# A split-precision attention block on one core: part of its weight and bias loads issued by GpSimd in place of SyncE, and two numbers of the order tables

## The chip, the cores and the metric

The kernel runs on one core of a Trainium2 chip. The metric is the device time of one execution in microseconds (us). A core has five engines that run their own instruction streams in parallel: PE (TensorE; its weight loads are listed as PEld), DVE (VectorE), ACT (ScalarE), POOL (GpSimd) and SP (SyncE, which here only issues DMA transfers). DMA transfers run beside them.

## The reference

```python
h = rms_norm(x, norm_gain)                       # x: 2048 tokens x 1024
qa, ka, va, qb, kb, vb, ga, gb, mg = split(h @ w_in)
ya = banded_attention(rms(qa), rms(ka), va, 128, stride 1, bias, sink)   # 8 heads, 2 kv heads
yb = softmax-weighted sum over 3 groups of banded_attention(...)          # (window, dilation)
#    = (128, 1), (512, 4), (2048, 16), 8 heads each
ya, yb = ya * silu(ga), yb * silu(gb)
gates = sigmoid(mg + b_merge)
merged = gates[0] * (ya @ w_branch_a) + gates[1] * (yb @ w_branch_b)
out = x + merged @ w_out
```

All of it is in float32. The kernel reaches that accuracy on PE with pairs of fp16 numbers: each operand is a high half and a low half, and a product takes three matmuls (high by high, high by low, low by high).

## The kernel before

**Three stages.** In the first 80 us x is loaded, normalised, transposed and split into XH and XL, which stay in SBUF, and the gates of branch A are made. From 80 to about 1232 us the attention runs, with the gates of branch B and pieces of other work between. From there to the end is the tail: merge gates, the two branch projections and the output projection, as seven-product matrix multiplications.

**Units and pairs.** The attention is cut into 14 units (two of kind A, twelve of kind B, in the order A, B, A, B, B, B ...), each a group of heads with weights of its own (1024 x 384, float32, 1.5 MB) and a bias table (768 KB for A, 256 KB for B). A unit has 8 pairs, each two blocks of 128 tokens: 112 pairs of about 10 us. For a pair PE makes q, k and v (L693). ACT, DVE and POOL then norm q and k: ACT squares them, DVE sums, POOL refines the reciprocal root (L266 to L269), DVE scales (L753), POOL multiplies by the gain (L760), ACT makes the high halves (L766), DVE the low ones (L770), POOL copies them swapped (the "swap" copy, L775, into the tile spl). SP then issues a transpose through DMA, kq<-spl (L783 for A, L786 for B). PE makes the scores from kq (L846), DVE adds the bias and takes maxima (L861), ACT and DVE make the probabilities in two halves (L874, L878), SP issues their transpose, pt<-p (L884), and PE multiplies them by v (L895). POOL also sets a column of each v tile (L722, "vt") and works on the merging of heads (L1037, L1058), whose operands come by a load zz<-zd (L904).

**Weights.** The raw float32 weights of the unit after the present one go into the one raw tile, wraw, by four DMAs of 384 KB, in two twos (w_load, L180). ACT squares them (L215), PE sums (L191), DVE makes a scale from the sum, ACT makes the high halves and DVE the low ones (L238). After that the raw tile is free; from unit 3 on, eight units each put 1 MB of the branch and output weights there for a sum of squares (window, piece_load L1083 and L1086, piece_square L1090), before the next unit's weights come. Bias tables are loaded at the start of a unit (bias_load, L664 and L667). In the tail the same raw tile takes the merge gates' weights, "gate weights" below.

**What sets the order.** Each engine executes its instructions in the order in which the program writes them. In the attention that is set by a heap: at(t, f) places a step at a time counted in pairs, and tables hold the times (NORM for the steps of the norm, W_STEP for the weights: loads .1 and .6 pairs after a unit's start, squares from 1.9 on). W_SOON is subtracted from the loads' and squares' times for one unit alone, number 2, the second A unit. In the tail a planner places the steps by estimated times; G_LD is the lag that it assumes between the start and the landing of the first gate weights, and so decides when their squares and the matmul that sums them are written.

**DMAs.** Every DMA above is issued by SP, so that all are on one queue. SP's stream is in order: a transpose behind a load is issued after it.

Of the kernel before, what the change touches and what calls it, by code (L numbers as in the profile page):

```python
# [45 lines left out]
def unit_order():  # L46
    us = [("A", 0, 0)]
    for p in range(4):
# [9 lines left out]
NU = len(UNITS)  # L58
# [10 lines left out]
Y_PART = (-0.02, 0.571, 0.797, 0.981, 1.031)  # L69
GATE = (-0.062, 0.084, 0.255)  # L70
W_STEP = (0.1, 0.6, 1.9, 0.445, 4.186, 0.117, 0.301)
W_SOON = (1.9, .5)
W_MAX = (3.542, 3.596)
G_PREP = (5.907,)
N_PREP = (5.948, 6.756, 7.277)
# [4 lines left out]
            sum=.76, yl=7.0, cp=.66, pl=6.0, a2=.44, h2=.51, l2=.5)  # L80
SEQ = ((1, 0), (1, 1), (8, 0), (8, 1), (2, 0), (2, 1), (9, 0), (9, 1), (3, 0), (3, 1), (10, 0), (10, 1), (4, 0), (4, 1),
       (5, 0), (5, 1), (6, 0), (6, 1), (7, 0))
G_T0, G_LD, G_SQ = 5.0, 3.0, 2.0
W_RAW, L_LAST = 14.0, 0.4
STD, W_EARLY, G_TH, G_SI, G_CP, K_AT = 5.2, 24.0, 2.0, 4.0, 1.0, (4, 17)
Y_S = 4.0
# [24 lines left out]
def block_kernel(tc, x, w_units, w_gate, w_mrg, w_out, w_bra, w_brk, gain, qkg, sink, bias_a, bias_b, b_merge, out):  # L111
    nc = tc.nc
# [52 lines left out]
    def raw_tile():  # L165
        return wp.tile([128, NCH, 384], F32, name="wraw", bufs=1)
# [7 lines left out]
    def w_load(u, parts=(0, 1, 2, 3)):  # L174
        if u not in wtiles:
            wtiles[u] = [raw_tile()]
        raw = wtiles[u][0]
        src, n = (w_units[u], 384) if u < NU else (w_mrg[u - NU], 256)
        for i in parts:
            nc.sync.dma_start(out=raw[:, 2 * i:2 * i + 2, :n], in_=src[:, 2 * i:2 * i + 2, :])  # L180


    held = [False, True]
# [366 lines left out]
    n = 0  # L550
    for k in X_LD:
        for i in range(4 if k == "u" else 1):
            f, args = {"g": (gain_load, ()), "u": (w_load, (0, (i,)))}.get(k, (x_load, (k,)))
            if k in ("w0", "w1"):
                f, args = g_load, (int(k[1]),)
            at(.001 * n, f, *args)
            od.end["ld", k, i] = us_["land"] + us_["next"] * n
            n += 1
            if n == 8:
                at(.001 * n, small_loads)  # L560
    od.add("gs", "V", us_["gs"], [("ld", "g", 0)], 0, gain_scale)
    for t in range(NT):
# [9 lines left out]
        for h in range(2):  # L572
            k = 2 * t + h
# [53 lines left out]
    class Unit:  # L627
# [31 lines left out]
        def bias_load(self):  # L659
            big = self.u % 2 == 0  # L660
            b = bp.tile([128, 4, N_BIAS_A] if big else [128, 4, 128], F32, name=f"b{self.u % 2}")
            if self.kind == "A":
                self.bias = b
                nc.sync.dma_start(out=b[:], in_=bias_a[self.idx])  # L664
            else:
                self.bias = b[:].rearrange("p a b -> p (a b)")[:, :2 * N_BIAS_B].rearrange("p (a b) -> p a b", a=2)
                nc.sync.dma_start(out=self.bias[:], in_=bias_b[self.idx, self.g])  # L667

        def bias_scale(self):
            V.tensor_scalar(self.bias[:], self.bias[:], NSIG[self.br][:], None, OP.mult)  # L670
# [403 lines left out]
    pre = {}  # L1074
# [5 lines left out]

    def piece_load(u, k):
        if k < 4:
            nc.sync.dma_start(out=pre[u][1], in_=w_bra[k])  # L1083
        else:
            h, i = divmod(k - 4, 2)
            nc.sync.dma_start(out=pre[u][1].rearrange("p (a b) -> p a b", b=512), in_=w_out[h, :, 4 * i:4 * i + 4, :])  # L1086

    def piece_square(u, k, half):
        v = pre[u][1][:, 1024 * half:1024 * half + 1024]
# [87 lines left out]
    def w_forms(u, t):  # L1177

        r = []

        def split():
            raw, s, inv, _, _ = wtiles[u]
            wh, wl = (w[:].rearrange("p (f c n) -> p f c n", f=7, c=4) for w in wfull[u])
            v = raw[:, :, :256]
            r.extend((s, *w_sums(v[:, 0:4, 0:128], v[:, 0:4, 128:256], v[:, 4:8, 0:128], v[:, 4:8, 128:256],
                                 lambda t: t[:].rearrange("p (c n) -> p c n", c=4), lambda: sb_p.tile([128, 512], F32, name="sr")), wh, wl))
            wtiles[u, "forms"] = wh, wl
            std_im(u - NU)

        def hi(i):  # L1190
            A.activation(r[3][:, i], r[1][i], AF.Copy, scale=r[0][:])

        def lo(i):
            V.scalar_tensor_tensor(r[4][:, i], r[1][i], r[0][:], r[3][:, i], OP.mult, OP.subtract)

        at(t + F_AT[0], split)
        for i in range(4):
            at(t + F_AT[0] + .01 + F_AT[1] * i, lambda i=i: r[2][i]())
        for i in range(7):
            at(t + F_AT[2] + F_AT[3] * i, hi, i)  # L1200
            at(t + F_AT[2] + F_AT[3] * i + F_AT[4], lo, i)
        at(t + F_AT[5], w_load, NU + SEQ[2][0])
# [8 lines left out]
    for u in range(NU + 1):  # L1211
        t = 8 * u
        ahead = W_SOON if u == 1 else (0.0, 0.0)
        steps = [(t + W_STEP[i] - ahead[0], w_load, u + 1, (2 * i, 2 * i + 1)) for i in range(2)]
        for i in range(4):
            steps.append((t + W_STEP[2] + W_STEP[3] * i - ahead[1], w_square, u + 1, i))
            if u < NU:
                steps += [(t + W_STEP[4] + W_STEP[3] * i, w_hi, u + 1, i),
                          (t + W_STEP[4] + W_STEP[5] + W_STEP[3] * i, w_lo, u + 1, i)]
        chain(steps + [(t + d, f, u + 1) for d, f in zip(W_MAX, (w_sum, w_pow))])  # L1220

    for k in range(8):
        u = 3 + k
        t = 8 * u
        at(t + G_PREP[0] - .01, window, u)
        at(t + N_PREP[0], piece_load, u, k)
        for half in range(2):
            at(t + N_PREP[1 + half], piece_square, u, k, half)
# [7 lines left out]
    while t < NPAIR or heap or any(k >= t for k in fill):  # L1236
        u, j = divmod(t, 8)
# [676 lines left out]
    class Branch(Seven):  # L1914
        n, mm_us = 7, MM1
# [65 lines left out]
    class Out(Seven):  # L1981
        n, mm_us = 7, MM
# [77 lines left out]
    for s in range(8):  # L2060
        p = pos[0]
# [92 lines left out]
```

## Time and profile before

| | |
|---|---|
| time, median of 3 runs (lowest to highest) | 1905.94 us (1905.17 to 1907.07) |
| the profiled execution's own time; its span | 1904.35 us; 1902.3 us |
| PE, DVE, ACT, POOL busy | 98%, 79%, 66%, 30% of the span |
| granted clock of PE | 1.00 |
| DMA engines busy, mean of the attention | 0.84 |
| weight loads of the units (L180): number, size, time to landing | 56, 384 KB, 4.8 us |
| bias loads of B (L667) | 12, 256 KB, 3.6 us |

The profile lists, for groups of instructions, busy time and the idle time of the engine ahead of them with what ended it (the releaser). The chain of waits follows the work that ended last back from the end. A timeline row has start, busy time, engine, line, operation, tile written <- tiles read, sizes and count, and in brackets the idle time ahead with its releaser. SPq stands for the issuing of DMAs by SP.

### The profile page before, as it was taken

The page shows a single profiled execution, that of the slowest core. Times are in us where ns is not written, and L with a number is a line of the kernel's source. Part 1 is how long each engine was busy: PE and PEld are TensorE (multiplying, and loading weights), DVE is VectorE, ACT ScalarE, POOL GpSimd, SP SyncE. Part 2 cuts the span into 40 slices and gives each one's busy share as a digit, 9 for nine tenths or more (in the row PEclk, how much of TensorE's full clock was granted, in tenths as well). Part 3 has the DMA queues.
Part 4 walks back from the last instruction along what each step waited for, and adds up shares of the span by engine and source line. Part 5 has one row for each costly group of instructions (what it writes and reads, how often), then busy time and mean ns, then how long its engine had stood idle before and what let it go on. Part 6 is the DMA issues. An engine that isn't in the chain of part 4 may idle for free.

```text
span 1902.3 us, 51104 instructions
## 1 busy us (share of the span) xinstructions
PE 1869.9 (98%) x19254; PEld 1439.0 (76%) x19254; DVE 1499.3 (79%) x3837; ACT 1249.5 (66%) x3015; POOL 579.6 (30%) x1363
## 2 busy tenths in 40 slices
PE   6999999999999999999999999999999999999999
PEld 4567987889999899998999899544444446776775
DVE  7689879986886888878789888748779644987885
ACT  8477768886777776777777766565666865433341
POOL 0133433443463435544454444300000000322121
PEclk9999999999999999999999999999999999999999
DMA  6259998988888679878897777776666648854452
GB/s 257 83 107 199 168 198 138 201 163 156 168 149 180 139 158 201 146 165 173 145 176 149 147 148 134 170 303 183 204 199 188 192 150 272 297 164 120 144 151 74
DMA packets 638983, 326.21 MB, mean 171 GB/s; under 512 B 458768, under 2 KB 589712, under 8 KB 636304
## 3 DMA queue, kind: packets, MB, share of 16 engines
q1 hardware_dynamic: 638592, 322.69, 73.4%
q8 instruction: 150, 2.46, 0.6%
q14 instruction: 97, 0.79, 0.1%
q10 hardware_dynamic: 144, 0.26, 0.0%
HBM read 139.08 MB, written 73.66 MB: 112 GB/s over the span
## 4 chain that ended last, share of the span: by engine, by line
PE 89%; DMA 5%; ACT 2%; DVE 2%; issue 1%; POOL 0%; SPq 0%; DVEq 0%; POOLq 0%; ACTq 0%
PE pj L693 42%; PE fps L1607 18%; PE fps L1927 8%; PE fps L2012 7%; PE s L846 5%; PE pv L895 4%; DMA pt<-p 2%; DMA kq<-spl 2%; PE pj L306 2%; PE pj L354 1%; PE fps L306 1%; ACT jk L443 1%; PE pt L959 1%; DMA bigl<-sd 1%; PE s L484 0%
## 5 line engine op out<-in xcount | busy, mean ns | idle before, releaser
L693 PE MATMUL pj<-wl,XH 128*128 128x128 f16 (+2 forms) x2816 | 715.2, 268 | 0.0
L693 PE MATMUL pj<-wh,XL 128*128 128x128 f16 (+2 forms) x2816 | 711.7, 269 | 0.0
L693 PE MATMUL pj<-wh,XH 128*128 128x128 f16 (+2 forms) x2816 | 708.6, 268 | 0.0
L693 PEld LDWEIGHTS <-XH 128*128 128x128 f16 x5632 | 574.9, 112 | 54.2
L693 PEld LDWEIGHTS <-XL 128*128 128x128 f16 x2816 | 315.8, 112 | 23.8
L861 DVE CUSTOM_DVE_ANT_0 pr<-s,b,ubuf 128x256 f32<-128x256 f32 (+3 forms) x512 | 219.0, 465 | 40.7 <-PE s L846 38.1
L878 DVE SCALAR_TENSOR_TENSOR p<-pr,p 128x512 f16<-128x512 f32 (+2 forms) x256 | 194.9, 761 | 47.9 <-ACT p L874 46.4
L760 POOL TENSOR_TENSOR rw<-rw,g 128x128 f32<-128x128 f32 (+1 forms) x224 | 149.2, 686 | 195.2 <-DVE rw L753 174.8
L1937 POOL TENSOR_TENSOR g<-g,t 128x512 f32<-128x512 f32 x32 | 48.4, 1512 | 522.1 <-DVE t L1859 521.6
L1607 PEld LDWEIGHTS <-wh 128*128 128x128 f16 x1064 | 104.2, 99 | 123.5 <-issue 0.5
L711 ACT ACTIVATE rw<-pj 128x256 f32<-128x256 f32 (+1 forms) x224 | 87.4, 390 | 134.5 <-PE pj L693 134.0
L775 POOL COPY spl<-spl 128x256 f16<-128x256 f16 (+1 forms) x224 | 96.4, 459 | 244.6 <-DVE spl L770 244.6
L874 ACT ACTIVATE p<-pr 128x512 f16<-128x512 f32 (+2 forms) x256 | 157.6, 616 | 11.9 <-DMA pt<-p 7.4
L846 PE MATMUL s<-kq 128*128 128x128 f16 (+1 forms) x1984 | 151.3, 217 | 5.9 <-DMA kq<-spl 4.7
L1927 PE MATMUL fps<-y,bigh 128*128 128x128 f16 x1792 | 153.4, 219 | 0.0
L1927 PE MATMUL fps<-y,bigl 128*128 128x128 f16 x896 | 151.7, 219 | 0.0
L846 PEld LDWEIGHTS <-kq 128*128 128x128 f16 x2016 | 131.0, 98 | 22.2 <-issue 7.2
L2012 PE MATMUL fps<-WO,mf 128*128 128x512 f16 x660 | 147.5, 379 | 0.0
L1927 PEld LDWEIGHTS <-bigh 128*128 128x128 f16 x1792 | 139.0, 98 | 7.3
L895 PE MATMUL pv<-vt,pt 128*128 128x65 f16 (+1 forms) x2784 | 131.6, 193 | 4.3 <-DMA pt<-p 4.1
L895 PEld LDWEIGHTS <-pt 128*128 128x128 f16 x3024 | 119.5, 97 | 19.6 <-DMA pt<-p 7.1
L766 ACT ACTIVATE spl<-rw 128x512 f16<-128x512 f32 (+1 forms) x112 | 72.0, 643 | 79.1 <-POOL vt L722 67.2
(255 smaller groups left out, 3803.5 us busy)
## 6 DMA issues: line engine op xcount, KB each, us to landing
wraw<-in_w_units_dram SPq DMA_DIRECT2D x56, 384.0 KB, 4.8
g<-mgd SPq DMA_DIRECT2D x64, 256.0 KB, 5.0
wraw<-in_w_mrg_dram SPq DMA_DIRECT2D x45, 256.0 KB, 4.3
mgd<-t SPq DMA_DIRECT2D x43, 256.0 KB, 2.8
zd<-z SPq DMA_DIRECT2D x128, 66.0 KB, 2.1
zz<-zd SPq DMA_DIRECT2D x64, 132.0 KB, 3.3
xt<-in_x_dram SPq DMA_DIRECT2D x16, 512.0 KB, 7.8
ytd<-yo SPq DMA_DIRECT2D x32, 256.0 KB, 3.3
```

Source lines behind the costliest of these rows:

```text
L693: out.append(lambda lhs=lhs, rhs=rhs, ch=ch, a=a, b=b, k=k: T.matmul(ps[:, a:b], lhsT=lhs[:, ch, :], rhs=rhs[:, ch, a:b], start=(k == 0), ...
L711: A.activation(self.rw[:, n * i:n * i + n], self.ps[i][:, :n], AF.Copy)
L760: G.tensor_tensor(q[:, i, :un.nq, :], q[:, i, :un.nq, :], g, OP.mult)
L775: G.tensor_copy(sp[:, i, nh:, :, :], sp[:, i, nq:nh, ::-1, :])
L846: T.matmul(self.sv[j][:, o:o + k1 - k0], lhsT=q[:, h, :], rhs=kt[:, un.nq + kh + v * un.nk, k0:k1], start=(v == 0), stop=(v == 1))
L861: V.tensor_tensor_reduce(out=self.pv[:, j, self.p0:self.p0 + W], in0=self.sv[j], in1=un.bias[:, self.h0 + j, self.b0:self.b0 + W], scale=I ...
L874: A.activation(self.sp[:, :128 * n], self.pr, AF.Copy, scale=PSC)
L878: V.scalar_tensor_tensor(self.sp[:, 128 * n:], self.pr, PSC, self.sp[:, :128 * n], OP.mult, OP.subtract)
L895: T.matmul(self.po[:, j, :w], lhsT=p[:, n * j + s, :], rhs=un.v[key][:, vh, c0:c0 + w], start=(k == 0 and s == 0), stop=(k == 2 and s == n ...
L1607: T.matmul(b[k][:], lhsT=w[:, i, ch, :], rhs=xform(PROD[i][0], lo, ch, q), start=(i < 3 and n == 0), stop=(n == 11), skip_group_check=True)
L1927: out.append(lambda p=p, c=c, wl=wl, yl=yl, n=n: T.matmul(ps[:, 128 * p:128 * p + 128], lhsT=w[wl][:, i, c, p, :], rhs=y[:, yl, c, :], sta ...
L2012: out.append(lambda p=p, ml=ml, wl=wl, k=k: T.matmul(ps[:], lhsT=m[:, ml, p, :], rhs=WO[:, i, wl, p, :], start=(fresh and k == 0), stop=(k ...
```

## The change

Three edits. W_SOON goes from (1.9, .5) to (0, 0): unit 2's loads come 1.9 pairs later, its squares half a pair later, as those of every other unit. G_LD goes from 3.0 to 6.0. And 74 DMAs are issued by GpSimd in place of SP: the weights of units 1 to 13 (52), the bias tables (14) and the eight pieces of 1 MB. The weights of unit 0 and the gate weights of the tail stay with SP.

```diff
-W_SOON = (1.9, .5)
+W_SOON = (0.0, 0.0)
...
-G_T0, G_LD, G_SQ = 5.0, 3.0, 2.0
+G_T0, G_LD, G_SQ = 5.0, 6.0, 2.0
...  w_load
         for i in parts:
-            nc.sync.dma_start(out=raw[:, 2 * i:2 * i + 2, :n], in_=src[:, 2 * i:2 * i + 2, :])
+            (nc.gpsimd if 0 < u < NU else nc.sync).dma_start(out=raw[:, 2 * i:2 * i + 2, :n], in_=src[:, 2 * i:2 * i + 2, :])
...  bias_load
-                nc.sync.dma_start(out=b[:], in_=bias_a[self.idx])
+                nc.gpsimd.dma_start(out=b[:], in_=bias_a[self.idx])
...
-                nc.sync.dma_start(out=self.bias[:], in_=bias_b[self.idx, self.g])
+                nc.gpsimd.dma_start(out=self.bias[:], in_=bias_b[self.idx, self.g])
...  piece_load
         if k < 4:
-            nc.sync.dma_start(out=pre[u][1], in_=w_bra[k])
+            nc.gpsimd.dma_start(out=pre[u][1], in_=w_bra[k])
         else:
             h, i = divmod(k - 4, 2)
-            nc.sync.dma_start(out=pre[u][1].rearrange("p (a b) -> p a b", b=512), in_=w_out[h, :, 4 * i:4 * i + 4, :])
+            nc.gpsimd.dma_start(out=pre[u][1].rearrange("p (a b) -> p a b", b=512), in_=w_out[h, :, 4 * i:4 * i + 4, :])
```

The first place is SP's stream at the first two pairs of unit 5, a B unit (at 510 us in the trace of before). Before, the bias load (b) and the four weight loads stand between the transposes:

```order
L884 DMA_TRANSPOSE pt_9544<-p_9481 128x8x128
L667 DMA b_9557<-in_bias_b_dram 128x512
L180 DMA wraw<-in_w_units_dram 128x768 x2
L904 DMA zz<-zd_82 128x2x132 x2
L786 DMA_TRANSPOSE kq<-spl 128x6x128 x2
L884 DMA_TRANSPOSE pt_9675<-p_9602 128x8x128
L180 DMA wraw<-in_w_units_dram 128x768 x2
L976 DMA ytd<-yo 128x512
L884 DMA_TRANSPOSE pt_9788<-p_9723 128x8x128
```

Now the same stretch of SP's stream is:

```order
L884 DMA_TRANSPOSE pt_9544<-p_9481 128x8x128
L904 DMA zz<-zd_82 128x2x132 x2
L786 DMA_TRANSPOSE kq<-spl 128x6x128 x2
L884 DMA_TRANSPOSE pt_9675<-p_9602 128x8x128
L976 DMA ytd<-yo 128x512
L884 DMA_TRANSPOSE pt_9788<-p_9723 128x8x128
L904 DMA zz<-zd_82 128x2x132 x2
```

The five loads are gone from it; each kq and pt is the next DMA behind what was ahead of the loads.

The second place is the same stretch on POOL. Before, from the gain of unit 5's first pair to the gain of its second:

```order
L760 TENSOR_TENSOR rw<-rw,g_857 128x128 x2
L722 MEMSET vt 128x2
L775 COPY spl<-spl 128x256 x2
L266 TENSOR_TENSOR rs_t<-rs_y 128x8
L267 TENSOR_TENSOR rs_t<-rs_t,qss 128x8
L268 TENSOR_SCALAR rs_t<-rs_t 128x8
L269 TENSOR_TENSOR qr<-rs_t,rs_y 128x8
L1058 TENSOR_TENSOR zz<-zz,bm_e 128x4x64 x3
L722 MEMSET vw 128x2
L1037 COPY zz<-nmB 128x4
L760 TENSOR_TENSOR rw<-rw,g_857 128x128 x2
L722 MEMSET vt 128x2
```

Now:

```order
L760 TENSOR_TENSOR rw<-rw,g_857 128x128 x2
L667 DMA b_9557<-in_bias_b_dram 128x512
L722 MEMSET vt 128x2
L180 DMA wraw<-in_w_units_dram 128x768 x2
L775 COPY spl<-spl 128x256 x2
L266 TENSOR_TENSOR rs_t<-rs_y 128x8
L267 TENSOR_TENSOR rs_t<-rs_t,qss 128x8
L268 TENSOR_SCALAR rs_t<-rs_t 128x8
L269 TENSOR_TENSOR qr<-rs_t,rs_y 128x8
L1058 TENSOR_TENSOR zz<-zz,bm_e 128x4x64 x3
L722 MEMSET vw 128x2
L180 DMA wraw<-in_w_units_dram 128x768 x2
```

The bias load and two weight loads stand ahead of the swap copy L775 of the first pair, and the other two ahead of the merge's copy L1037 (which comes next there) and the gain L760 of the second.

The third place is PE at the start of the tail, where matmuls on XH and XL (the first product) are followed by those on bigh and bigl (sums of blocks of h, loaded from DRAM). The norm matmul L191 sums the squares of the first gate weights of the planner. Before:

```order
L1607 MATMUL fps<-XL,wh 128x512
L1607 LDWEIGHTS wl
L1607 MATMUL fps<-XH,wl 128x512
L191 MATMUL fps<-wsq,ones 128x4
L1607 LDWEIGHTS wh
L1607 MATMUL fps<-bigh,wh 128x512
L1607 LDWEIGHTS wh
L1607 MATMUL fps<-bigl,wh 128x512
L1607 LDWEIGHTS wl
```

Now, twelve matmuls later:

```order
L1607 MATMUL fps<-bigh,wh 128x512
L1607 LDWEIGHTS wh
L1607 MATMUL fps<-bigl,wh 128x512
L1607 LDWEIGHTS wl
L1607 MATMUL fps<-bigh,wl 128x512
L191 MATMUL fps<-wsq,ones 128x4
L1607 LDWEIGHTS wh
L1607 MATMUL fps<-bigh,wh 128x512
L1607 LDWEIGHTS wh
```

L191 went from ahead of the first twelve matmuls on bigh and bigl to behind them. DVE and ACT change by a few rows there.

## The prediction

> **What bounds the kernel now.** First the head of the profile, with the busy shares, then the DMA queues and issues.
>
> ```profile
> span 1902.3 us, 51104 instructions
> PE 1869.9 (98%) x19254; PEld 1439.0 (76%) x19254; DVE 1499.3 (79%) x3837; ACT 1249.5 (66%) x3015; POOL 579.6 (30%) x1363
> q1 hardware_dynamic: 638592, 322.69, 73.4%
> wraw<-in_w_units_dram SPq DMA_DIRECT2D x56, 384.0 KB, 4.8
> wraw<-in_w_bra_dram SPq DMA_DIRECT2D x4, 1024.0 KB, 6.1
> kq<-spl SPq DMA_TRANSPOSE x208, 3.6
> ```
>
> PE is busy 98% of the span, so an edit gains only what it takes out of the 32 us in which PE is not busy, and loses only where it makes PE wait. Nearly all bytes go through one queue, q1, which SP fills; the loads that the change moves (384 KB and 1024 KB) stand in it beside the transposes (pt and kq) that the attention waits for. The table by stage says where PE is idle: preparation, attention, the passage to the tail, the tail. After the time its columns are PE, PEld, DVE, ACT, POOL (us, instructions), granted clock, DMA share and GB/s.
>
> ```profile
> 0.00:80.00 80.00, 62.05 (x333) 37.78 (x334) 59.26 (x120) 57.94 (x107) 1.96 (x10) 1.00 0.44 170
> 80.00:1230.00 1150.00, 1139.84 (x13815) 1014.25 (x13813) 961.86 (x2805) 839.23 (x2246) 507.27 (x1305) 1.00 0.84 162
> 1230.00:1250.00 20.00, 18.91 (x88) 8.27 (x86) 9.25 (x20) 12.10 (x23) 0.00 (x0) 1.00 0.90 327
> 1250.00:1899.00 649.00, 649.00 (x5024) 378.67 (x5022) 468.43 (x892) 340.20 (x640) 70.33 (x48) 1.00 0.60 185
> PE s L846 <- DMA kq<-spl: 4.7, 5, 1.4
> PE pv L895 <- DMA pt<-p: 4.1, 5, 1.3
> ```
>
> The clock is full throughout. Of 1150 us of attention PE is idle for 10.2, and the last two rows (PE's waits in that stretch: total, times, longest) say for what: 4.7 + 4.1 = 8.8 us for transposes. That is the most the attention can give. The tail after 1250 has no idle time at all, and the passage has 1.1 us. The 18 us at the start end before the first moved load matters. Which of the ten waits stand behind a moved load is read from PE's timeline (start, busy, then in brackets the idle time ahead and its releaser) and SP's.
>
> ```profile
> 150.56 0.61 PE L846 MATMUL s<-kq 128*128 128x128 f16 x8 [1.42 <-DMA kq<-spl]
> 152.77 0.41 PE L895 MATMUL pv<-vt,pt 128*128 128x65 f16 x8 [1.12 <-DMA pt<-p]
> 180.72 0.44 PE L895 MATMUL pv<-vt,pt 128*128 128x65 f16 x9 [1.35 <-DMA pt<-p]
> 500.53 0.49 PE L846 MATMUL s<-kq 128*128 128x128 f16 x6 [0.94 <-DMA kq<-spl]
> 530.75 0.44 PE L846 MATMUL s<-kq 128*128 128x128 f16 x5 [1.01 <-DMA kq<-spl]
> 745.37 0.49 PE L846 MATMUL s<-kq 128*128 128x128 f16 x6 [0.44 <-DMA kq<-spl]
> 970.28 0.49 PE L846 MATMUL s<-kq 128*128 128x128 f16 x6 [0.94 <-DMA kq<-spl]
> ```
>
> ```profile
> 142.41 1.37 SPq L180 DMA_DIRECT2D wraw<-in_w_units_dram  x2
> 143.83 2.62 SPq L783 DMA_TRANSPOSE kq<-spl  x1
> 146.63 5.42 SPq L884 DMA_TRANSPOSE pt<-p  x2
> ...
> 489.93 0.35 SPq L1083 DMA_DIRECT2D wraw<-in_w_bra_dram  x1
> ...
> 493.61 5.37 SPq L786 DMA_TRANSPOSE kq<-spl  x2
> ...
> 511.66 0.57 SPq L667 DMA_DIRECT2D b<-in_bias_b_dram  x1
> 512.28 2.45 SPq L180 DMA_DIRECT2D wraw<-in_w_units_dram  x2
> ...
> 515.81 2.56 SPq L786 DMA_TRANSPOSE kq<-spl  x2
> 518.47 1.25 SPq L884 DMA_TRANSPOSE pt<-p  x1
> 519.77 1.06 SPq L180 DMA_DIRECT2D wraw<-in_w_units_dram  x2
> ```
>
> A transpose behind a load is issued late and lands late: 142.41 loads, then the kq and pt of 143.83 and 146.63, and PE waits at 150.56 and 152.77. The same pattern precedes 500.53 (a 1 MB load at 489.93) and 530.75 (loads at 512.28 and 519.77).
>
> **The change, part by part.** The working is against the profiled execution's own 1904.35 us (span 1902.3 and 2.05 around it); the median of the runs shown, 1905.94, is 1.59 more, which is added at the end.
>
> *Unit 2's loads (W_SOON).* They leave 142 and 152, so the two waits there should go: -(1.42 + 1.12) = **-2.5**, at worst 0. They come back 1.9 pairs later, around 163 and 171, and run beside transposes near the 1.35 wait at 180.72. I charge **+1.0** there; the ends are 0 and the +2.5 that the same four loads cost at 142. The squares on them start half a pair later; nothing waits, since unit 2's weights are needed a whole unit on.
>
> *The other loads leave SP's queue.* The waits at 500.53, 530.75, 745.37 and 970.28 add to 0.94 + 1.01 + 0.44 + 0.94 = 3.33. I take **-3.0** (ends -3.3 and 0): the transposes are then issued at once, yet share the 16 engines with the same bytes, so a rest stays.
>
> *What POOL pays.* No row shows a load issued by POOL. SP's direct loads cost it 1.06/2 = 0.53 us each, its transposes 1.25, and if POOL were held until the load landed it would be the 4.8 of the issues. So c, POOL's time for one issue, lies between 0.53 and 4.8; I take 1.0, between the two issue costs, since a plain load is an issue and not a transfer on its engine. POOL's timeline shows the cover:
>
> ```profile
> 492.96 0.74 POOL L775 COPY spl<-spl 128x256 f16<-128x256 f16 x2 [1.87 <-DVE spl L770]
> ...
> 512.27 0.74 POOL L775 COPY spl<-spl 128x256 f16<-128x256 f16 x2 [2.47 <-DVE spl L770]
> ...
> 518.83 1.17 POOL L760 TENSOR_TENSOR rw<-rw,g 128x128 f32<-128x128 f32 x2 [1.16 <-DMA zz<-zd]
> ...
> 522.91 0.74 POOL L775 COPY spl<-spl 128x256 f16<-128x256 f16 x2 [2.86 <-DVE spl L770]
> ```
>
> In a unit's first pair, a bias load and two weight loads go ahead of the swap copy L775, where POOL idles 2.47: 3c = 3.0 makes the copy 0.5 late. That copy ends at 512.27 + 0.74 = 513.01, while SP issues its kq only at 515.81, 2.80 later, behind the loads. With these gone the copy may be 2.80 late before kq is later than now: c can reach (2.47 + 2.80)/3 = **1.76** free of charge. In the second pair two loads stand ahead of L760: 2c = 2.0 against 1.16, and the 0.84 over it falls into the 2.86 of idle time ahead of 522.91. A piece load is c = 1.0 against 1.87. So **0**, with the loss beyond 1.76 kept as a rival.
>
> *Waits that come to POOL with the loads.* Each waits for the raw tile; behind it on POOL are the vt memset, the swap copy, and the kq transpose that waits for the copy.
>
> ```profile
> 69.47 1.01 DVE L238 SCALAR_TENSOR_TENSOR wl<-wraw,ubuf,wh 128x768 f16<-128x768 f32 x1
> 89.81 0.20 POOL L266 TENSOR_TENSOR rs_t<-rs_y 128x10 f32<-128x10 f32 x1 [26.83 <-ACT rs_y L258]
> 488.85 1.01 DVE L238 SCALAR_TENSOR_TENSOR wl<-wraw,ubuf,wh 128x768 f16<-128x768 f32 x1
> 498.24 1.05 ACT L1090 ACTIVATE wraw<-wraw 128x1024 f32<-128x1024 f32 x1
> ```
>
> The tile is free when the last low half is made: at 70.48 for unit 1, with POOL idle until 89.81, and at 489.86 for the 1 MB piece, before POOL reaches its idle time at 492.96 - 1.87 = 491.09, where the piece load now stands. So no wait. That piece, issued about 491.1 + 1.0 and landing 6.1 later, comes at 498.2, just as ACT's square at 498.24 wants it; a little lateness there holds ACT, not PE, whose 500.53 wants kq.
>
> *The tail (G_LD).* The only PE row that moves is the norm matmul of the first gate weights, now behind the twelve matmuls on bigh and bigl.
>
> ```profile
> 1241.60 0.39 PE L191 MATMUL fps<-wsq,ones 128*128 128x4 f32 x2 [0.99 <-ACT tq L1457]
> 1237.82 9.92 DMA bigl<-sd
> 1247.79 25.84 PE fps L1607 x119
> ```
>
> PE waits 0.99 there for the squares. But the chain of waits does not run through it: it goes through the last bigl landing at 1247.74, after which PE never idles. Taking the norm away moves the matmuls on bigh and bigl earlier, and they then wait for their landings instead. **0**, with -1.0 as the other end.
>
> Sum: 1904.35 - 2.5 + 1.0 - 3.0 + 0 + 0 = 1899.85; with 1.59, **1901.4**.
>
> Two rules of the Trainium skill speak against parts of this. "DMA: Bandwidth & Descriptors", section "Issuing engines are not separate DMA queues", says that loads from any engine end on the same 16 DMA engines, so that another issuer saves only issue time; the trace's one queue cannot show it, and by it the -3.0 would shrink to little: that is the second rival. "SBUF — State Buffer", section "SBUF: two separate sides", says that a load issued by GpSimd needs descriptors written by GpSimd, which is locked out while VectorE runs in a two-port mode, and gives 620 ns alone and 3100 ns beside VectorE; an estimate from that page is 3 x 3.1 = 9.3 us against 5.27 of cover, and 12 times the difference, 48 us, for the kernel. No run here shows it; the first rival is priced without it.
>
> **The rivals.**
>
> *POOL held by its issues (slower).* The place is L775 in the first pair of each unit; it decides from c = 1.76. At c = 2.5: 3 x 2.5 - 2.47 - 2.80 = 2.23 us that kq lands later than now, at each of the 12 unit starts whose loads stand so (units 1 to 12, each loading its own bias and the next unit's weights): +26.8. The kq gains are then gone, those at 150 remain: 1904.35 - 2.5 + 26.8 + 1.59 = **1930**. For it: DVE is busy 962 of the 1150 us beside POOL, and no row bounds c below 1.76. Against it: both issue costs that the trace has are lower, and PE may have more slack than I grant.
>
> *The engines stay shared (no change).* The DMA engines are busy 0.84 of the attention, and the moved bytes are the same. If collisions only move (a kq at 500 instead of one at 530), the -3.0 becomes 0 and +1.0 becomes +2.5: 1904.35 - 2.5 + 2.5 + 1.59 = **1906**. For it: the pt wait at 180.72 and others stand behind no load. Against it: every kq wait does.
>
> *The tail's wait goes too (faster).* The 0.99 is really saved: 1901.4 - 1.0 = **1900.4**. Against it stands the chain through bigl.
>
> **How the numbers follow.** About 0.2% (3.8 us) is what a measurement of this kernel can tell from no change, so faster is below 1902.1 and slower above 1909.8. The forecast has 0.40; its own range runs from 1899.1 (-2.5, 0, -3.3, -1.0) to 1902.9 (+2.5 in place of +1.0), so 0.30 of it is faster and 0.10 the same. The tail case has 0.07, faster. Engines shared has 0.23, the same. POOL held has 0.30: 0.18 up to the price at c = 2.5, 0.12 above. Faster 0.37, same 0.33, slower 0.30. The range goes down to the attention's whole 8.8 (1904.35 - 8.8 + 1.59 = 1897.1) and up to 1930, which leaves out about 0.12 above and little below.
>
> **What would show it.** Right: the waits at 150, 500, 530, 745 and 970 are gone, kq is issued within 0.3 us of its copy, and POOL's rows at 512 have at most 0.5 us of new lateness. Wrong by POOL: idle time ahead of L775 that "issue" or a load ends, kq's issue waiting for L775 for over 2.8 us, and new PE waits for kq in the first pair of every unit. Wrong by shared engines: kq is issued early, but its time to landing grows past the 3.6. At the tail PE should wait for bigh or bigl in place of L191.

## The result, and the profile after

The change makes the kernel slower: 1923.79 us, median of five runs (1920.9 to 1952.06), against 1905.94; the ratio is 1.0116 with a 95% interval of 1.0094 to 1.0138. The ratio is that of the means, without the longest run, which is over 1.5% above the fastest. The forecast was 1901.4, on the other side of no change. The profiled execution of the changed kernel is that longest one (1952.06 us, mean clock 0.991); a second profile of the same kernel (1931.25 us) is used beside it.

The head of the profile after, its DMA queues and its DMA issues:

```profile
span 1950.3 us, 51177 instructions
PE 1882.9 (97%) x19254; PEld 1445.1 (74%) x19254; DVE 1500.0 (77%) x3837; ACT 1247.9 (64%) x3015; POOL 619.9 (32%) x1437
q1 hardware_dynamic: 627936, 289.13, 67.8%
q0 software_dynamic: 6560, 33.56, 6.7%
wraw<-in_w_units_dram POOLq DMA_DIRECT2D x52, 384.0 KB, 7.0
wraw<-in_w_out_dram POOLq DMA_DIRECT2D x4, 1024.0 KB, 8.3
kq<-spl SPq DMA_TRANSPOSE x208, 3.7
```

The 74 loads, 33.56 MB, are now on a queue of their own, q0. POOL has 74 more entries and 40.3 us more busy time: 40.3/74 = 0.54 us for one issue, at the lower bound of the prediction (0.53). The unit weights now take 7.0 us to land in place of 4.8. The median transpose hardly changed (3.6 to 3.7), which hides what happened to a few. PE's waits say it (line, what it waited for, total, times, longest):

```profile
PE s L846 <- DMA kq<-spl: 22.5, 6, 7.8
PE pv L895 <- DMA pt<-p: 21.7, 8, 5.5
```

8.8 us of waits for transposes became 44.2, so 35.4 more; PE's busy time went from 1869.9 to 1882.9, 13.0 more. Together that is 48.4 of the 48.0 us by which this span is longer. The second profile gives the same account, with waits of 19.8 + 7.1 = 26.9 (18.1 more) and 1879.1 busy (9.2 more) against a span 27.2 longer:

```profile
span 1929.5 us, 51177 instructions
PE 1879.1 (97%) x19254; PEld 1443.7 (75%) x19254; DVE 1502.9 (78%) x3837; ACT 1246.9 (65%) x3015; POOL 621.1 (32%) x1437
PE s L846 <- DMA kq<-spl: 19.8, 7, 5.5
PE pv L895 <- DMA pt<-p: 7.1, 6, 2.5
```

One site shows the mechanism. Here is POOL, then SP, then PE in the changed kernel around 1080 us, where a B unit starts:

```profile
1075.43 0.59 POOL L667 DMA_DIRECT2D b<-in_bias_b_dram  x1
1076.03 0.13 POOL L722 MEMSET vt<- 128x2 f16 x1
1076.07 1.06 POOL L180 DMA_DIRECT2D wraw<-in_w_units_dram  x2
1077.58 0.74 POOL L775 COPY spl<-spl 128x256 f16<-128x256 f16 x2 [0.45 <-DVE spl L770]
...
1081.60 1.14 POOL L180 DMA_DIRECT2D wraw<-in_w_units_dram  x2
```

```profile
1078.00 5.87 SPq L786 DMA_TRANSPOSE kq<-spl  x2
...
1090.13 8.11 SPq L884 DMA_TRANSPOSE pt<-p  x1
```

```profile
1089.71 0.33 PE L693 MATMUL pj<-wl,XH 128*128 128x384 f16 x1
...
1097.98 0.69 PE L846 MATMUL s<-kq 128*128 128x128 f16 x6 [7.79 <-DMA kq<-spl]
1098.47 0.52 PE L693 MATMUL pj<-wh,XL 128*128 128x384 f16 x1
```

Before, SP issued the same two kq here, behind the bias load and two weight loads:

```profile
1041.14 2.67 SPq L786 DMA_TRANSPOSE kq<-spl  x2
```

The swap copy L775 is not held: POOL still waits 0.45 us for DVE ahead of it. SP issues the first kq at 1078.00, while the second copy still runs, and no load stands ahead of it. The second kq, issued at 1079.75, takes 18.19 us to land (the row in the chain of waits is below), and PE stands for 7.79. Before, the same two took 4.92 and 4.24 us from their issue, and PE did not wait. The loads that run beside it, issued at 1076.07 and 1081.60, land 9.7 to 15.8 us after issue. SP is held too: one pt issue takes 8.11 us of its time.

```profile
1079.75 18.19 DMA kq<-spl
```

The same stretch by 20 us, with all engines, the granted clock, the DMA share and GB/s as the last three columns:

```profile
1060.00:1080.00 20.00, 20.00 (x265) 19.60 (x263) 16.92 (x43) 13.62 (x39) 10.39 (x28) 1.00 0.88 152
1080.00:1100.00 20.00, 12.21 (x105) 10.09 (x104) 8.26 (x24) 5.79 (x16) 5.62 (x13) 0.81 1.19 151
1100.00:1120.00 20.00, 20.00 (x174) 16.79 (x173) 17.22 (x53) 15.97 (x44) 9.14 (x25) 0.93 0.79 145
1120.00:1140.00 20.00, 20.00 (x173) 17.58 (x172) 17.59 (x54) 14.98 (x42) 8.16 (x22) 1.00 0.57 101
```

The DMA engines are busier (1.19 against 0.88) and move no more (151 GB/s against 152); before, the 20 us at this place (1043 to 1063) have a share of 1.14 and move 205 GB/s. And the granted clock falls to 0.81 in the stretch of the wait and is 0.93 in the next: a matmul of 128x384 that took 0.33 us ahead of the wait takes 0.52 behind it. So this wait is paid a second time, in PE's longer busy time, the other part of the loss. Not each wait is: behind one of 3.53 us at 179.52 the clock stays at 1.00.

The pattern over the whole attention, worked out from the DMA records of each execution: a transpose is "beside" when its time from issue to landing overlaps that of a moved load.

| | transposes beside: median, over 8 us, longest | transposes apart: median, longest | GB/s (DMA share) while a moved load is in flight |
|---|---|---|---|
| before | 4.75, 1 of 110, 8.3 | 3.20, 5.9 | 235 (1.04) |
| after | 6.20, 33 of 110, 20.1 | 3.19, 6.5 | 196 (1.03) |
| after, second profile | 6.09, 26 of 109, 16.1 | 3.20, 6.4 | 210 (1.04) |

Transposes apart from the loads are untouched. Of those beside them a quarter to a third now takes over 8 us, and the engines, as busy as before, move less.

### The profile page after: what moved, and what is told of

It is laid out like the page before. It is cut to its first block, busy times and chain, and to the rows that moved or that the text cites. A ratio compares the mean times of both kernels' runs of the same rounds, so it can differ in the third digit from the quotient of the medians.

```text
span 1950.3 us, 51177 instructions
## 1 busy us (share of the span) xinstructions
PE 1882.9 (97%) x19254; PEld 1445.1 (74%) x19254; DVE 1500.0 (77%) x3837; ACT 1247.9 (64%) x3015; POOL 619.9 (32%) x1437
## 3 DMA queue, kind: packets, MB, share of 16 engines
q0 software_dynamic: 6560, 33.56, 6.7%
q8 instruction: 150, 2.46, 0.6%
## 4 chain that ended last, share of the span: by engine, by line
PE 87%; DMA 7%; DVE 2%; ACT 2%; issue 1%; SPq 0%; POOL 0%; DVEq 0%; POOLq 0%
PE pj L693 40%; PE fps L1607 17%; PE fps L1927 8%; PE fps L2012 7%; PE s L846 5%; PE pv L895 4%; DMA pt<-p 4%; DMA kq<-spl 3%; PE pj L354 2%; PE pj L306 2%; PE fps L306 1%; PE pt L959 1%; DVE pr L861 1%; PE s L484 0%; DMA bigl<-sd 0%
## 5 line engine op out<-in xcount | busy, mean ns | idle before, releaser
L1937 POOL TENSOR_TENSOR g<-g,t 128x512 f32<-128x512 f32 x32 | 48.4, 1513 | 521.5 <-DVE t L1859 519.7
L760 POOL TENSOR_TENSOR rw<-rw,g 128x128 f32<-128x128 f32 (+1 forms) x224 | 148.8, 685 | 189.4 <-DVE rw L753 177.2
L775 POOL COPY spl<-spl 128x256 f16<-128x256 f16 (+1 forms) x224 | 96.9, 461 | 230.5 <-DVE spl L770 230.5
```

What stands on the lines that cost most here:

```text
L760: G.tensor_tensor(q[:, i, :un.nq, :], q[:, i, :un.nq, :], g, OP.mult)
L775: G.tensor_copy(sp[:, i, nh:, :, :], sp[:, i, nq:nh, ::-1, :])
```

## The experiments

Three theories stood at the start. **Mixing**: transposes on SP's queue and loads on GpSimd's queue slow each other when in flight together. **POOL**: the issues delay the swap copy. **Tables**: W_SOON or G_LD cost the time. Ratios are against the kernel before on the same chip.

**1. Tables alone.** All loads stay with SP.

```diff
-W_SOON = (1.9, .5)
+W_SOON = (0.0, 0.0)
-G_T0, G_LD, G_SQ = 5.0, 3.0, 2.0
+G_T0, G_LD, G_SQ = 5.0, 6.0, 2.0
```

> The kernel before with the two table edits alone (W_SOON and G_LD), every load still issued by SP. Three theories. Mixing: transposes on SP's queue and loads on GpSimd's queue slow each other when they run at once. POOL: the loads' issue time on GpSimd delays the swap copies. Tables: the later place of unit 2's loads and of the tail's first norm matmul costs the time. Mixing and POOL expect 1902 to 1907 us (ratio 0.998 to 1.0005), with the PE waits at 150 us gone and no wait over 2 us. Tables expects at least 1915.

Measured: 1904.81 us, ratio 0.9995 (0.9987 to 1.0004). Tables falls. PE's waits for transposes are 5.1 + 2.6 = 7.7 in place of 8.8: of the two at 150 there is one of 0.16 left, and one of 2.46 stands at 197.59, so the expectation that none would be over 2 us was off. (The pt behind that wait was issued at 190.37, when unit 2's loads had all landed, and run 13, without the table edits, has a wait of 2.24 for the same pt: so it need not come from the edit.) At the tail the wait is now for bigl, as foretold:

```profile
197.59 0.71 PE L895 MATMUL pv<-vt,pt 128*128 128x65 f16 x18 [2.46 <-DMA pt<-p]
...
1242.51 0.38 PE L1607 MATMUL fps<-bigl,wh 128*128 128x512 f16 x1 [0.65 <-DMA bigl<-sd]
```

**2. Queue alone.** All 74 loads by GpSimd, both tables as before.

```diff
-W_SOON = (0.0, 0.0)
+W_SOON = (1.9, .5)
-G_T0, G_LD, G_SQ = 5.0, 6.0, 2.0
+G_T0, G_LD, G_SQ = 5.0, 3.0, 2.0
```

> All 74 loads issued by GpSimd, both tables as before. Mixing and POOL expect 1917 to 1926 us (ratio 1.006 to 1.011), with PE waits of 3 us or more for kq or pt in several units whose loads are in flight. Tables expects 1906. Mixing expects in those units transposes that take 10 us or more from issue to landing though they were issued on time; POOL expects transposes that are issued late, behind a late swap copy, and land in about 3.6.

(The diff is against the changed kernel.) Measured: 1947.67 us, ratio 1.0231 (1.0193 to 1.0268): twice the loss of the whole change, more than any theory expected. 38 of 109 transposes beside a load took over 8 us, the longest 21.0. So the loss is the queue's, and the table edits, worth nothing by themselves, save half of it. That they do so by moving unit 2's loads is read from the waits near the old place, 4.76 and 7.80 us here and 5.63 and 8.82 in run 9; W_SOON was not tried alone.

**3. Weights alone**, and **4. bias tables and pieces alone**, on GpSimd, tables as before.

```diff
 # 3: weights
-            nc.sync.dma_start(out=raw[:, 2 * i:2 * i + 2, :n], in_=src[:, 2 * i:2 * i + 2, :])
+            (nc.gpsimd if 0 < u < NU else nc.sync).dma_start(out=raw[:, 2 * i:2 * i + 2, :n], in_=src[:, 2 * i:2 * i + 2, :])
 # 4: bias_load and piece_load, two lines each, as here
-                nc.sync.dma_start(out=b[:], in_=bias_a[self.idx])
+                nc.gpsimd.dma_start(out=b[:], in_=bias_a[self.idx])
```

> Of the queue move only the 52 weight loads (20 MB), bias tables and pieces on SP, tables as before. Mixing expects most of the loss, 1914 to 1923 us, since the waits of the changed kernel stand beside weight loads. POOL, by number of issues, expects 52/74 of about 17 us: 1918. The share of the loss is compared with the next run's.

> Of the queue move only the 14 bias tables and the 8 pieces (13 MB), weights on SP, tables as before. Mixing expects a small loss or none, 1904 to 1910 us, since these transfers are single and shorter than four weight loads in a row. POOL expects 22/74 of about 17 us: 1911.

Measured: 1924.68 us, 1.0101 (1.0088 to 1.0114), and 1917.23, 1.0057 (1.0045 to 1.007). Both are above the ranges that Mixing gave, the first by 1.7 us. In the first, PE's long waits stand at 146, 158 and 377 us alone; no wait over 0.6 us lies between 400 and 1200. Neither splits POOL from Mixing.

**5. POOL's time alone.** Loads with SP; beside each, GpSimd issues one DMA of 4 bytes.

```diff
+    def tiny():
+        i = dcount[0] % 40
+        dcount[0] += 1
+        nc.gpsimd.dma_start(out=dum[:, i:i + 1], in_=b_merge[0:1, 0:1])
...
+            if 0 < u < NU:
+                tiny()
...  and tiny() beside each bias load and each piece load
```

> The kernel before, all loads by SP, and beside each of the 74 loads one more DMA of 4 bytes issued by GpSimd into a spare tile, at the places where the changed kernel issues its loads. POOL pays the issues, but nothing of size is in flight on its queue. POOL expects the loss of the queue move, 1920 us or more. Mixing expects 1904 to 1908 us, no transpose beside a load over 9 us.

Measured: 1906.26 us, ratio 1.0003 (0.9994 to 1.0013). The engine row and the issues of that run:

```profile
PE 1873.8 (98%) x19254; PEld 1441.3 (76%) x19254; DVE 1498.6 (79%) x3837; ACT 1249.7 (66%) x3015; POOL 620.1 (33%) x1437
dum<-in_b_merge_dram POOLq DMA_DIRECT2D x74, 0.0 KB, 3.1
```

POOL carries the same 620 us and 1437 entries as in the changed kernel, and nothing is lost. The POOL theory falls. Run 5 does not have a load's wait for its tile; in the changed kernel POOL has one such wait, ahead of the first bias table (78.5 us, at the start, where it stood idle before as well).

**6. Half the load.** Like run 2, with each weight load cut in two of 192 KB.

```diff
-            (nc.gpsimd if 0 < u < NU else nc.sync).dma_start(out=raw[:, 2 * i:2 * i + 2, :n], in_=src[:, 2 * i:2 * i + 2, :])
+            e = nc.gpsimd if 0 < u < NU else nc.sync
+            for a in (2 * i, 2 * i + 1) if e is nc.gpsimd else (2 * i,):
+                d = 1 if e is nc.gpsimd else 2
+                e.dma_start(out=raw[:, a:a + d, :n], in_=src[:, a:a + d, :])
```

> All loads by GpSimd, tables as before (like the run with the queue move alone, 1947.7 us), but each 384 KB weight load cut into two of 192 KB, one chunk each: the same bytes and packets of half the size, twice the issues. If a transpose waits for whole load packets in turn, half the size halves what mixing costs: 1920 to 1932. If the mixing cost goes by bytes in flight, 1940 to 1955. POOL (104 issues more of 0.55 us) expects over 1955.

Measured: 1938.05 us, ratio 1.0166 (1.0139 to 1.0193), between the two answers. The records show that the edit did not do what was meant: the weights' packets went from 6144 bytes to 4608 (3328 of them) and 3072 (1664 of them), not all to half. The loss shrank from 2.3% to 1.7%, with twice the weight issues; the two intervals meet at 1.0193.

**7. Spread.** The changed kernel with one weight load at a time.

```diff
-        steps = [(t + W_STEP[i] - ahead[0], w_load, u + 1, (2 * i, 2 * i + 1)) for i in range(2)]
+        steps = [(t + .1 + .4 * i - ahead[0], w_load, u + 1, (i,)) for i in range(4)]
```

> The changed kernel with the four weight loads of a unit issued by GpSimd one at a time, at .1, .5, .9 and 1.3 pairs after the unit's start, in place of two and two at .1 and .6. Bytes and issues are the same. If the cost comes from several loads in flight at once on the second queue beside transposes, it shrinks: 1906 to 1913 us, and fewer than 10 transposes over 8 us. If it goes by bytes or by issues, it stays at 1918 to 1926.

Measured: 1928.29 us, ratio 1.0118 (1.0096 to 1.014), the same as the change. There are 19 transposes over 8 us in place of 33 (longest 12.3), but more of them are beside a load (149 in place of 110). But 57 of the 69 loads behind 100 us still overlap another load in flight (60 of 69 in the changed kernel), so the run did not take the bursts apart, and whether they matter stays open.

**8. Late weights** (units 5 to 13) and **9. early weights** (units 1 to 4) on GpSimd, all else as before.

```diff
 # 8
+            (nc.gpsimd if 4 < u < NU else nc.sync).dma_start(out=raw[:, 2 * i:2 * i + 2, :n], in_=src[:, 2 * i:2 * i + 2, :])
 # 9
+            (nc.gpsimd if 0 < u < 5 else nc.sync).dma_start(out=raw[:, 2 * i:2 * i + 2, :n], in_=src[:, 2 * i:2 * i + 2, :])
```

> The kernel before with only the weights of units 5 to 13 issued by GpSimd, the rest and the tables as before. In the run with all weights on GpSimd the long waits stood at 146, 158 and 377 us alone, beside transposes of the A units (384 KB each), and none after 400. If that holds, this version keeps the gain (the kq waits at 530, 745 and 970 go) without the loss: 1902 to 1905 us. If a load on the second queue costs wherever it is, 1912 or more.

> The kernel before with only the weights of units 1 to 4 issued by GpSimd; the complement of the run with units 5 to 13. In the kernel before the DMA engines are busy 1.03 to 1.10 of the stretches 128 to 210 and 333 to 374 us, where these loads run, and 0.6 to 1.0 later. If saturated engines are what turns the second queue into PE waits, this version has all of the loss of the run with all weights (1.0101): 1920 to 1928 us, waits near 146, 158 and 377. If the loss goes by number of loads, 16 of 52: 1911.

Measured: run 8 1903.31 us, ratio 1.0 (0.9984 to 1.0015); run 9 1922.04, ratio 1.0096 (1.0076 to 1.0115). The 16 early loads hold all of the loss of the 52. Waits of run 9, then PE's total waits of run 8:

```profile
152.42 1.16 PE L895 MATMUL pv<-vt,pt 128*128 128x65 f16 x18 [5.63 <-DMA pt<-p]
165.71 1.01 PE L846 MATMUL s<-kq 128*128 128x128 f16 x8 [8.82 <-DMA kq<-spl]
```

```profile
PE pv L895 <- DMA pt<-p: 3.4, 6, 1.1
PE s L846 <- DMA kq<-spl: 2.4, 3, 1.7
```

One thing that differs from early to late is in the profile of *before*, read by stretches of about half a unit (the last two columns are the DMA share and GB/s):

```profile
128.00:169.00 41.00, 37.71 (x515) 28.63 (x514) 37.36 (x91) 33.56 (x78) 16.11 (x34) 1.00 1.03 191
169.00:210.00 41.00, 39.05 (x637) 38.35 (x634) 38.90 (x102) 34.60 (x82) 15.87 (x33) 1.00 1.10 191
251.00:292.00 41.00, 41.00 (x435) 30.36 (x433) 29.09 (x83) 28.87 (x78) 15.96 (x49) 1.00 0.93 182
333.00:374.00 41.00, 41.00 (x533) 34.53 (x531) 38.45 (x100) 35.13 (x82) 18.48 (x37) 1.00 1.08 205
497.00:538.00 41.00, 39.05 (x551) 37.94 (x549) 34.81 (x117) 27.28 (x77) 22.72 (x58) 1.00 1.01 185
579.00:620.00 41.00, 41.00 (x433) 37.64 (x432) 28.56 (x79) 29.19 (x80) 14.55 (x47) 1.00 0.84 169
```

Of the early loads those that stand at 142 and 349 in before have the long waits of run 9 behind them; they run in stretches at 1.03 and 1.08, and beside an A unit's transposes. The early loads at 260 (0.93) have none, and in 579 to 620, with room left, no run shows a wait for a transpose of over 0.6 us. The share is no rule: in 497 to 538, at 1.01, run 8 has the four weight loads on GpSimd too and no wait for a transpose of over 0.3 us, and the 2.82 us at 476 in the first profile after belongs, by its instruction, at 451 of before, in a stretch (415 to 456) at 0.87. Nor does any run separate the share from the kind of unit. Run 8 has 3 us of transpose waits less than before, but its time cannot be told from it.

**10. Bias tables added to run 8.**

```diff
+                (nc.gpsimd if self.u > 3 else nc.sync).dma_start(out=self.bias[:], in_=bias_b[self.idx, self.g])
```

> The version with the weights of units 5 to 13 on GpSimd, and the bias tables of units 4 to 13 (256 KB each) on GpSimd too. With all loads on GpSimd there were waits at 524, 755 and 985 us, in stretches where the DMA engines are busy 0.98 to 1.01 before; with weights alone there were none. If three loads in a row on the second queue are what it takes there, waits of 2 to 5 us come back at these three places: 1910 to 1918 us. If a bias table adds nothing, 1902 to 1906.

Measured: 1908.62 us, ratio 1.0022 (1.0005 to 1.0038), between the two answers: no wait is over 1.6 us, and by the instruction that waits only the one at 755 came back (1.51 at 731); those at 524 and 985 are at most 0.4. More transposes are slow, though: 9 of 114 beside a load take over 8 us (longest 11.0), in run 8 it is 2 of 116 (longest 9.0). That three loads in a row are what it takes is not shown.

**11. Pieces alone on GpSimd.**

```diff
-            nc.sync.dma_start(out=pre[u][1], in_=w_bra[k])
+            nc.gpsimd.dma_start(out=pre[u][1], in_=w_bra[k])
...  and the same for w_out
```

> The kernel before with only the eight pieces of 1 MB issued by GpSimd. If they are the loss of the run with bias tables and pieces (1.0057), waits of 2 to 4 us stand at 499, 727 and 953: 1911 to 1918 us. If the bias tables were it, 1904 to 1907.

Measured: 1926.35 us, ratio 1.0106 (1.0091 to 1.0121). Eight DMAs cost as much as the whole change, at the three places named:

```profile
506.16 0.49 PE L846 MATMUL s<-kq 128*128 128x128 f16 x6 [3.79 <-DMA kq<-spl]
736.74 0.80 PE L846 MATMUL s<-kq 128*128 128x128 f16 x6 [3.92 <-DMA kq<-spl]
968.47 0.80 PE L846 MATMUL s<-kq 128*128 128x128 f16 x6 [5.54 <-DMA kq<-spl]
```

At the first, the piece is issued at 493.76 and lands 10.72 us later; the pt that SP issues at 493.57 takes 11.2, and the next kq 9.46. In before, the piece took 5.73, the pt, issued behind it, 8.28, and that kq 6.88. That this run is slower than run 4, which moves the bias tables as well, shows that the parts do not simply add.

**12. The changed kernel again**, unedited, is the second profile used above.

> The changed kernel once more, for a profile of an execution whose clock is not as low as 0.991. About 1922 us, PE waits for kq and pt of 25 to 35 us in all in place of 8.8, GpSimd's issue 0.55 us each, kq issued on time.

Measured: 1931.25 us in one run, 26.9 us of waits. The expected 1922 was too low for this execution.

**13. Pieces in four DMAs of 512 columns** and **14. pieces .4 pairs later**, both on GpSimd and against run 11.

```diff
 # 13
+            for j in range(4):
+                nc.gpsimd.dma_start(out=pre[u][1][:, 512 * j:512 * j + 512], in_=w_bra[k][:, 512 * j:512 * j + 512])
...  and the same for w_out
 # 14
-N_PREP = (5.948, 6.756, 7.277)
+N_PREP = (6.35, 7.16, 7.6)
```

> The eight pieces of 1 MB alone on GpSimd, each cut into four DMAs of 256 KB (512 columns), so that its packets are a quarter of 8 KB and the issues are four times as many, with 2.4 us of GpSimd per piece against the 1.87 of idle time ahead of the swap copy. If the size of the packets is what holds the transposes, the loss of the uncut pieces (1.0106) shrinks to less than half: 1906 to 1914 us. If it is the sharing of the engines by two queues, whatever the size, 1918 to 1928.

> The eight pieces alone on GpSimd, uncut, .4 pairs (4 us) later, with their squares as much later. The transfers are the same; the transposes that they run beside are others. If the place decides, the waits of 4.0, 4.1 and 5.7 us at 502, 733 and 963 change by more than half, either way. If it goes by bytes, they stay and the time is 1920 to 1928.

Measured: 1918.06 us, ratio 1.0062 (1.0044 to 1.008), and 1910.94, ratio 1.0027 (1.0017 to 1.0038). In run 13 the packets came out at 4096 bytes, half of 8192 and not a quarter, and the loss fell by two fifths. In run 14, with the same packets, it fell by three quarters. The three waits of run 11 are gone; the longest behind 500 us are these, of other instructions (before, two of them waited 0.44 at 745 and 0.94 at 970):

```profile
521.97 0.50 PE L846 MATMUL s<-kq 128*128 128x128 f16 x6 [1.42 <-DMA kq<-spl]
747.64 0.49 PE L846 MATMUL s<-kq 128*128 128x128 f16 x6 [1.16 <-DMA kq<-spl]
972.88 0.49 PE L846 MATMUL s<-kq 128*128 128x128 f16 x6 [1.57 <-DMA kq<-spl]
```

Which transposes a load runs beside matters; the size of its packets may, but run 13 has four times the issues as well.

The packet records say more of the place. Count, from the issue of a site's first moved load to the landing of its last, the half microseconds in which both at least 4 load packets and at least 20 transpose packets start. At the site of 1075 shown above that comes to 10.0 us in the changed kernel. In run 10 the same five loads are on GpSimd too; there it is 2.0 us, since the loads' packets go first and the transposes' after them, no transpose beside them takes over 6.7 us, and PE does not wait. In run 11 it is 3.5, 2.5 and 4.0 us at the three pieces with waits and at most 1.5 at the other five; in run 14 it is at most 2.0. So being in flight together is not enough: the long transposes come where the packets of the two queues take turns. This is a reading of the records and not a test, since a longer transfer also has more time to overlap, and what decides between the two cases is not shown.

## Why the prediction was wrong

**The step that failed** is "The other loads leave SP's queue": I took -3.0 "(ends -3.3 and 0)", on the ground that the transposes "are then issued at once, yet share the 16 engines with the same bytes, so a rest stays". They are issued at once. But 0 was no bound. On one queue the load ahead of a transpose costs it about the load's own time (before, 8.28 for the pt behind a piece of 5.73, where transposes apart take 3.20). On two queues both can go on at once and both finish late (pt 11.2 and the piece 10.72 in run 11), and less is moved in all (196 to 210 GB/s against 235). By itself the move costs 2.3% (run 2), 42 us between the medians, where I had a gain of 3. The prediction's "loses only where it makes PE wait" also left something out: 13.0 of the 48.0 us, and 9.2 of the 27.2 in the second profile, are PE's longer busy time.

**Unit 2's loads.** The -2.5 at 150 came (run 1). The +1.0, with 2.5 as its far end, was taken from those loads on SP's queue; there run 1 shows no wait that came with them (the one of 1.35 at 180.72 is 1.37 at 178.57), and its ratio, 0.9987 to 1.0004, holds no change and the -1.5 of both terms alike. On GpSimd's queue the new place has waits of 0.98, 1.79 and 3.53 us in the first profile, though it is still better than the old place, as the 1.0231 of run 2 against 1.0116 suggests:

```profile
167.47 0.71 PE L895 MATMUL pv<-vt,pt 128*128 128x65 f16 x18 [0.98 <-DMA pt<-p]
173.11 0.71 PE L895 MATMUL pv<-vt,pt 128*128 128x65 f16 x18 [1.79 <-DMA pt<-p]
179.52 0.71 PE L895 MATMUL pv<-vt,pt 128*128 128x65 f16 x18 [3.53 <-DMA pt<-p]
```

**What POOL pays**: 0, right (run 5), with c at 0.54 where I took 1.0. **The tail**: 0, right; the wait went over to bigl.

**The rivals.** The slower one had the right sign and the wrong mechanism: 1930 lies near the measured time, but it needed c over 1.76 and a late swap copy, and both runs and rows deny it (run 5). That the range, with 1930 as its upper end, holds the measured time is luck. The Trainium skill, "SBUF — State Buffer", section "SBUF: two separate sides", gives 3100 ns for a DMA issued by GpSimd beside a VectorE copy in a two-port mode; the prediction took it as time of the issue. Here, with DVE busy 77% of the span, none of the 74 issues takes over 0.72 us, so the estimate of 48 us does not hold for this case; whether DVE ran in such a mode no row shows. The second rival named the right place, the shared engines, and supposed that collisions "only move". They grow, and the sign that the prediction gave for it came: kq is issued early, and its time to landing goes from 3.6 to as much as 18.19. The rule behind it, "DMA: Bandwidth & Descriptors", section "Issuing engines are not separate DMA queues" in the Trainium skill, agrees with the trace as far as it goes: no bandwidth was gained (196 to 210 GB/s against 235). That something could be lost was to be seen in the profile before, in shares of 0.98 and over at most of the places with waits; a price it could not give, as run 8 shows.

**What stays open.** Why two queues together move less: a transpose's packet is 256 bytes and a load's on q0 4096 to 8192, and runs 6 and 13 point to the size, but neither made the packets as small as meant, and both changed the number of issues too. Whether it takes a second queue, or this one (software_dynamic in the profile, with packets twice as long for the weights), is not separated: a second queue of another issuer was not tried. That the parts do not add (run 4 against run 11) is unexplained. No version beats the kernel before beyond its interval; the lowest ratios are those of run 1 (0.9995) and run 8 (1.0).

## What to carry to other kernels

When a transfer stands in the way of another on one queue, a second queue (here GpSimd's) takes away the order and not the load: look at the DMA share of the very stretch where they meet, and be prepared for both to finish late where it is about 1. Whether they do has to be measured, site by site. Judge such a move by the longest transfer beside the moved ones and by who waits for it, since the median hardly changes. A step that only shifts a load by some microseconds may be worth nothing on one queue and 1% on the other.

## What the runs showed of the hardware

- A DMA issued by GpSimd cost it 0.50 to 0.72 us (mean 0.54 in both run 5, with 4 bytes each, and the changed kernel), and the 4 bytes landed after 3.1 us.
- While a moved load was in flight, the DMA engines moved 196 to 210 GB/s with loads and transposes on two queues, against 235 GB/s on one, at the same share (1.03 to 1.04).
- With a wait of PE of 7.8 us came a granted clock of 0.81 in that stretch of 20 us and 0.93 in the next, and matmuls of 0.52 us in place of 0.33; PE's busy time in the changed kernel's two profiles was longer by 13.0 and 9.2 us.
- The same weight loads had packets of 3072 bytes on SP's queue and 6144 on GpSimd's; the 1 MB pieces had 8192 on both.
